# Sums and products of the Hyena spectra, the branch sums, the decay subtraction and the filter sums moved from GpSimd to VectorE

## The chip, the cores and the metric

The kernel runs on one core of one Trainium2 chip. A core has a TensorE (PE in the profile) for matmuls, a VectorE (DVE), a ScalarE (ACT), a GpSimd (POOL), and a SyncE (SP) that here issues most of the DMAs. Each engine works through its own queue in order, and semaphores hold an instruction back until what it reads is ready.

The metric is the device time of one launch in microseconds, the median of several runs. Lower is better.

## The reference

Two layers of an encoder trunk on 512 tokens of width 1024, in float32. Each layer does:

```
hn = RMSNorm(h);  u = hn @ w_in, cut into the parts of three branches and three gates
y_a = attention(q, k, v)          8 query heads, 2 key/value heads, rotary positions
y_b = hyena(v, x1, x2)            two long convolutions over 1024 points, by FFT
y_c = gated linear attention      4 heads, forward and backward, with decay gates
mixed = sum_i sigmoid(gate_i) * (y_i @ w_branch_i)
h = h + mixed @ w_out
h = h + cross_attention(RMSNorm(h), RMSNorm(mem))
h = h + relu(RMSNorm(h) @ w1)^2 @ w2
```

Four places of it matter here. The Hyena convolution multiplies spectra:

```
y = irfft(rfft(u, n=2L) * spec, n=2L)[:L] + u * skip
```

Its filter comes from a small sine network, is windowed, and is divided by the sum of its absolute values before its own rfft. The decay gates are `g = log_sigmoid(logit) / 16`, of which running sums are taken. And `mixed` is a sum over three branches.

## The kernel before

**Tiles.** Activations stand transposed, channels on the 128 partitions and the 512 tokens along the free axis, so most tiles are 128x512 float32. A matmul in float32 is made of three matmuls on rounded halves (`mm3`, L251 to L253): high by high, low by high, high by low. Every operand is split first: ScalarE rounds a copy (`split`, L235: wh, xh, pqh, mixh), and VectorE subtracts it from the source to get the low half (L236: wl, xl, pql, mixl). Weights arrive in chunks of 128x1024 (`wr`), two buffers of them, and are split the same way into `wh` and `wl`, three buffers each; so each weight chunk passes ScalarE and VectorE before TensorE can use it.

**Order.** A layer is written as generators (attention `at`, its projections and splits, `gp` and `gh` for gated linear attention, `hy0` and `hy1` for the two channel halves of Hyena, `ga` for gates, `me0`, `me1`, `me2` for merging a branch, `wo`, `kv`). A list of names (ORDER0, ORDER) says in which order their steps are traced. From the trace a planner with a model of costs makes each engine's queue; priorities shift it (weight splits are pulled 200 places ahead by SPLIT_AHEAD, some matmuls are pushed back by LATE). The queue of each engine is fixed before the launch. So an instruction that waits holds all that stand behind it on its engine.

**The lines that the change touches.**

- ENGS (L170) gives letters to a few groups of elementwise operations: V for VectorE, P for GpSimd. `engs(key)` turns them into engines. `fq` is used by `quarters` (L618 to L622) in the filters, `hq` by `quarters` in Hyena, `hp` in the spectral products (L823 to L826), `hi` in the inverse step (L830 to L838), `mx` in the norm ahead of the layer.
- `quarters` makes four tiles out of even and odd halves: one sum (L618), one difference (L619), and two tiles in two halves of 128x256 each (L622).
- `spectral` runs twice for each half of the channels, so eight times in all. In each of its four groups g it multiplies the tile by the filter's spectrum F, which comes from DRAM by a DMA, in four operations: two products of 128x512 (L823, L824) and a difference and a sum of 128x256 (L825, L826). Then sums and differences go back (L830 to L834) and four results (L838) are split for the matmuls of the inverse transform. With the letters of before, a call puts on GpSimd both halves of one tile of `quarters` (L622), the four operations of group 2, and two of the four L838.
- `filters` has four rounds a layer (two convolutions by two channel halves). A round adds and subtracts two halves of w3 (L673, L674, from `w3r`, one buffer, filled by a DMA), sums absolute values into `acc` (L711, three times a round), and ends in `quarters` (fq: L618 and L619 on GpSimd). In layer 0 the filters lie beside attention; those of layer 1 lie in the MLP of layer 0.
- `gla_proj` subtracts for each of four heads `g - c` (L965), and two scans on VectorE read the result (L966, L968). `c` comes from ScalarE in one piece for all four heads.
- `merge` multiplies the gate by the branch on VectorE (L1116), then adds it to `acc` (L1117), eight times for each of two branches a layer. After the last branch the sum is split (mixh, mixl) for w_out.

GpSimd does more than that: sums of squares for the norms (L352), the rotary sum (L452), part of the last MLP sums (L1376, L1377), small copies of the decay (L973 to L982), and the DMAs of the transform matrices.

Of the kernel before, what the change touches and what calls it, by code (L numbers as in the profile page):

```python
# [15 lines left out]
ALU = mybir.AluOpType  # L16
# [77 lines left out]
def laid_out(a):  # L94
# [43 lines left out]
    for s_ in range(2):  # L138
# [28 lines left out]
LATE = dict(ff=50, fn=100, fr=100, fs=50, gA=100, gm=35, go=150, gq=35, gs=150, gt=10, hc=100, ht=150,  # L167
            kt=300, pt=100, pv=150, qt=200, xs=200, xt=35, xv=10)

ENGS = dict(fq='PPVV', hq='VVPV', hp='VVPV', hi='VVVVPVPV', lx='VVVVVVVV', aw='V',  # L170
            mx='VPVPVPVP')
SMALL = 768

# [1 line left out]
class Trunk:  # L175
# [461 lines left out]
    def filters(self, l):  # L637

        nc, I = self.nc, self.I
# [24 lines left out]
        for o in range(2):  # L664
            rn = self.rnbuf[2 * (l % 2) + o]
            self.rn[l].append(rn)
            for c in range(2):


                raw = self.t("w3r", (P, 2, 256), F32, "w3r")  # L670
                self.load(raw, I["hy_w3"][l, o, c])
                wr = self.t("F", (P, 2, 256), F32, "w3s")
                nc.gpsimd.tensor_tensor(wr[:, 0], raw[:, 0], raw[:, 1], op=ALU.add)  # L673
                nc.gpsimd.tensor_tensor(wr[:, 1], raw[:, 0], raw[:, 1], op=ALU.subtract)  # L674
                wh = self.t("s12", (P, 2, 256), F32R, "w3h")
                for r in range(2):
                    nc.scalar.copy(wh[64 * r:64 * r + 64], wr[0:64])
# [6 lines left out]
                acc = self.t("s12", (P, 2, 256), F32, "acc")[:, 0]  # L684
                skip = self.skip
                self.load(skip, I["hy_skip"][l, o, c])
                for par in (1, 0):
                    win = self.t("win", (P, 2, 256), F32, "win")
                    self.load(win, I["c_win"][c, par])
                    T4 = []  # L690
                    for a in range(2):
                        tt = 2 * par + a
                        tk = slice(tt * P, (tt + 1) * P)
                        ps = self.ps("b", (P, 2, 256))
                        nc.tensor.matmul(ps, hs[:, tk], wh, start=True, stop=False)
                        nc.tensor.matmul(ps, hb[:, tk], wl, start=False, stop=True)
                        E = self.t("F", (P, 2, 256), F32, "eo")
                        nc.vector.tensor_tensor(E, ps, win[:, a].unsqueeze(1).to_broadcast([P, 2, 256]),
                                                op=ALU.mult)
                        if tt == 0:  # L700

                            nc.vector.tensor_tensor(tap0, E[0:1, 0], E[0:1, 1], op=ALU.add)
                            nc.vector.tensor_scalar(E[0:1], tap0.unsqueeze(1).to_broadcast([1, 2, 256]), 0.5,
                                                    None, op0=ALU.mult)

                        ab = self.t("F", (P, 2, 256), F32, "abs")
                        nc.scalar.activation(ab, E, AF.Abs)
                        top = acc if tt == 2 else ab[:, 0]
                        nc.vector.tensor_tensor(top, ab[:, 0], ab[:, 1], op=ALU.max)
                        if tt != 2:  # L710
                            nc.gpsimd.tensor_tensor(acc, acc, top, op=ALU.add)  # L711
                        eh, el = self.split_new(E, "f8", (P, 2, 256), "eo")
                        m = dft[par + 2 * a]


                        for x in range(1 + par):
                            bank = self.ps("a", (P, 2, 256))
                            for d in range(2):
                                with self.late("ff"):
                                    self.mm3(bank[:, d], m[:, d ^ x, 0], m[:, d ^ x, 1], eh[:, d], el[:, d],  # L720
                                             d == 0, d == 1 and tt > 0)
                            T4.append(bank)
                    if par == 1:
                        odd = [self.tile_sum("f8", T4[x], self.hold("f8", T4[2 + x]), (ALU.add, ALU.subtract)[x])
                               for x in range(2)]
                    else:
                        held = self.hold("f8", T4[1])
# [167 lines left out]
    def gla_proj(self, l):  # L895
# [66 lines left out]
        self.load(reset, I["c_reset"])  # L962
        for h in range(4):
            g, c = gs[h], xs[:, h]
            nc.gpsimd.tensor_tensor(g, g, c, op=ALU.subtract)  # L965
            nc.vector.tensor_tensor_scan(c[0:64], reset[0:64], g[0:64], 0.0,  # L966
                                         op0=ALU.mult, op1=ALU.add)
            nc.vector.tensor_tensor_scan(c[64:128, ::-1], reset[64:128, ::-1], g[64:128, ::-1],  # L968
# [132 lines left out]
    def merge(self, l, i, W, last):  # L1101
        nc = self.nc
        y = (self.ya, self.yb, self.yc)[i]
        for mc in range(4):
            w = self.wchunk(W[l], mc, ng=1)
            for j in range(2):
                m = 2 * mc + j
                py = self.ps("mm")
                self.proj_cm(py, w, slice(j * P, (j + 1) * P), y)
                t = self.gate[i][m]  # L1110
                if i == self.first:
                    a = self.t("h8", name="acc")
                    nc.vector.scalar_tensor_tensor(a, t, 1.0, py, op0=ALU.add, op1=ALU.mult)
                    self.acc.append(a)
                else:
                    nc.vector.scalar_tensor_tensor(t, t, 1.0, py, op0=ALU.add, op1=ALU.mult)  # L1116
                    nc.gpsimd.tensor_tensor(self.acc[m], self.acc[m], t, op=ALU.add)  # L1117
                if last:
                    self.mixed.append(self.split_new(self.acc[m], "g", name="mix", lo_tag="s12"))
            yield  # L1120
# [337 lines left out]
```

## Time and profile before

| | us |
|---|---|
| median of 3 runs | 2281.23 (2280.59 to 2283.82) |
| the profiled execution, whole | 2285.21 |
| its span in the trace | 2283.4 |
| GpSimd: L1117, 32 operations | 50.6 busy, 1.589 each |
| GpSimd: L838, 16 operations | 29.0 busy, 1.822 each |
| GpSimd: L823, 8 operations | 21.7 busy, 2.712 each |
| GpSimd: L711, 24 operations of 128x256 | 21.6 busy, 0.901 each |
| VectorE: weight splits L236, 324 of 128x1024 | 415.1 busy, 1.284 each |

How to read it: a profile is of one execution, and sums from its rows are held against that execution's time. Busy time is the time in which an engine had an instruction running. PE's is near the span, so what counts beside it is when PE has nothing to do. A row of the timeline has the start, the duration, the engine, the line, the operation, the tiles written and read, and their shapes; in brackets stands how long the engine had been idle before, and what ended that. On VectorE a duration includes a tail that overlaps the next instruction, so the distance between two starts is the price of one in a full queue.

### The profile page before, as it was taken

To read this page: it belongs to the slowest core of one execution; us is meant where nothing else is said; L and a number is where in the kernel's file an instruction comes from. 1 tells how busy PE (TensorE), PEld (TensorE's weight loads), DVE (VectorE), ACT (ScalarE), POOL (GpSimd) and SP (SyncE) were. 2 spreads that over 40 slices of the span, in tenths; PEclk is the share of its full clock that TensorE was granted. 3 is DMA by queue.
4 is the path that set the end of the run, shared out by engine and by line. 5 is a ranking of instruction groups with operands and counts; after the bars stand their busy time and mean duration, and the time that the engine had idled before them with its cause. 6 is when DMAs were issued, how large, how long until landed. Compare 5 with 4: busy or idle time off the path is not lost.

```text
span 2283.4 us, 28957 instructions
## 1 busy us (share of the span) xinstructions
PE 2197.6 (96%) x11032; PEld 1831.6 (80%) x11032; DVE 1533.5 (67%) x2455; ACT 1001.0 (44%) x1623; POOL 422.6 (19%) x353
## 2 busy tenths in 40 slices
PE   7989999998899999999999989999989999999999
PEld 5877888786678878888887878887867888888887
DVE  7798855979665765766485685667886566344445
ACT  6666844332344544443335576343323444433231
POOL 1142101224220101111060230102252101000004
PEclk9999999999999999999999999999989999999999
DMA  6442123223143243433344211332232322333332
GB/s 236 136 139 83 56 84 116 65 83 106 59 148 112 63 127 102 134 120 100 100 155 146 94 51 56 91 117 74 77 109 91 130 75 74 102 99 95 98 94 95
DMA packets 80098, 233.56 MB, mean 102 GB/s; under 512 B 9174, under 2 KB 11222, under 8 KB 79960
## 3 DMA queue, kind: packets, MB, share of 16 engines
q1 hardware_dynamic: 76792, 225.95, 31.2%
q0 software_dynamic: 3168, 5.77, 0.9%
q8 instruction: 86, 1.41, 0.3%
q14 instruction: 52, 0.43, 0.1%
HBM read 214.91 MB, written 16.78 MB: 101 GB/s over the span
## 4 chain that ended last, share of the span: by engine, by line
PE 78%; DVE 14%; issue 3%; ACT 2%; DMA 2%; POOL 1%; SPq 0%; DVEq 0%; POOLq 0%; ACTq 0%
PE ps L251 24%; PE ps L253 24%; PE ps L252 24%; DVE wl L236 3%; PE ps L557 1%; DVE ts L823 1%; ACT wh L235 1%; PE ps L566 1%; DMA F<-F 1%; PE ps L568 1%; DVE u L824 1%; PE ps L544 1%; DVE ts L611 1%; PE ps L545 0%; DMA wr<-in_w_in_dram 0%
## 5 line engine op out<-in xcount | busy, mean ns | idle before, releaser
L236 DVE TENSOR_TENSOR wl<-wr,wh 128x1024 fp32r<-128x1024 f32 x324 | 415.1, 1284 | 244.0 <-ACT wh L235 239.7
L235 ACT CAST wh<-wr 128x1024 fp32r<-128x1024 f32 (+1 forms) x328 | 341.0, 1042 | 507.1 <-PE ps L252 424.2
L253 PE MATMUL ps<-xh,wl 128*128 128x512 f32 x1344 | 530.6, 395 | 17.5 <-DVE wl L236 17.5
L251 PE MATMUL ps<-xh,wh 128*128 128x512 f32 x1344 | 532.9, 397 | 4.2 <-ACT wh L235 3.9
L252 PE MATMUL ps<-xl,wh 128*128 128x512 f32 x1344 | 531.1, 395 | 0.0
L253 PEld LDWEIGHTS ps<-xh,wl 128*128 128x128 f32 x1344 | 254.6, 189 | 73.8 <-DVE wl L236 22.5
L251 PEld LDWEIGHTS ps<-xh,wh 128*128 128x128 f32 x1344 | 254.8, 190 | 58.2 <-ACT wh L235 5.5
L252 PEld LDWEIGHTS ps<-xl,wh 128*128 128x128 f32 x1344 | 254.9, 190 | 50.0
L253 PE MATMUL ps<-hdh,wl 128*128 128x512 f32 x512 | 199.4, 390 | 0.0
L252 PE MATMUL ps<-hdl,wh 128*128 128x512 f32 x512 | 199.4, 390 | 0.0
L251 PE MATMUL ps<-hdh,wh 128*128 128x512 f32 x512 | 199.2, 389 | 0.0
L1374 DVE TENSOR_TENSOR macc<-ps,macc 128x512 f32<-128x512 f32 x96 | 65.9, 690 | 89.1 <-PE ps L253 88.9
L252 PEld LDWEIGHTS ps<-hdl,wh 128*128 128x128 f32 x512 | 96.1, 188 | 19.9
L253 PEld LDWEIGHTS ps<-hdh,wl 128*128 128x128 f32 x512 | 96.1, 188 | 19.8
L251 PEld LDWEIGHTS ps<-hdh,wh 128*128 128x128 f32 x512 | 96.1, 188 | 19.7
L1376 POOL TENSOR_TENSOR macc<-macc,rb 128x512 f32<-128x512 f32 x16 | 23.5, 1469 | 398.4 <-DVE macc L1374 398.4
L251 PE MATMUL ps<-wh,xh 128*128 128x256 f32 x320 | 91.7, 286 | 0.0
L252 PE MATMUL ps<-wl,xh 128*128 128x256 f32 x320 | 91.5, 286 | 0.0
L253 PE MATMUL ps<-wh,xl 128*128 128x256 f32 x320 | 91.1, 285 | 0.0
L1358 DVE TENSOR_TENSOR rl<-rl 128x512 f32<-128x512 f32 x64 | 44.6, 697 | 64.8 <-ACT rl L1357 64.8
L352 POOL TENSOR_TENSOR hsum<-hsum,hsq 128x512 f32<-128x512 f32 x30 | 43.6, 1454 | 168.3 <-ACT hsq L350 168.3
L1357 ACT ACTIVATE rl<-ps 128x512 f32<-128x512 f32 x64 | 37.9, 592 | 77.9 <-PE ps L253 77.9
(405 smaller groups left out, 4522.1 us busy)
## 6 DMA issues: line engine op xcount, KB each, us to landing
wr<-in_mlp_w_dram SPq DMA_DIRECT2D x128, 512.0 KB, 3.6
wr<-in_w_in_dram SPq DMA_DIRECT2D x108, 512.0 KB, 3.7
wraw<-in_x_wv_dram SPq DMA_DIRECT2D x16, 512.0 KB, 5.5
wr<-in_x_wk_dram SPq DMA_DIRECT2D x16, 512.0 KB, 3.7
F<-ff SPq DMA_DIRECT2D x32, 256.0 KB, 3.2
F<-F SPq DMA_DIRECT2D x32, 256.0 KB, 4.9
wr<-in_w_out_dram SPq DMA_DIRECT2D x16, 512.0 KB, 3.6
wr<-in_x_wq_dram SPq DMA_DIRECT2D x16, 512.0 KB, 3.7
```

The costliest lines, as they stand in the source:

```text
L235: r = self.nc.scalar.copy(hi, src)
L236: (lo_eng or self.nc.vector).tensor_tensor(lo, src, hi, op=ALU.subtract)
L251: mm(out, lh, rh, start=start, stop=False, skip_group_check=True)
L252: mm(out, lh, rl, start=False, stop=False, skip_group_check=True)
L253: mm(out, ll, rh, start=False, stop=stop, skip_group_check=True)
L352: eng.tensor_tensor(self.hsum, self.hsum, sq, op=ALU.add)
L544: nc.tensor.matmul(s, QH[:, tk], K2, start=True, stop=False)
L557: nc.tensor.transpose(pt[:, k, i * P:(i + 1) * P], Pn[i][:, (2 * kp + k) * P:(2 * kp + k + 1) * P], self.ident)
L1357: nc.scalar.activation(r, ps, AF.Relu)
L1358: nc.vector.tensor_tensor(r, r, r, op=ALU.mult)
L1374: nc.vector.tensor_tensor(acc[m], ps, acc[m], op=ALU.add)
L1376: nc.gpsimd.tensor_tensor(acc[m], acc[m], rb, op=ALU.mult)
```

## The change

All operations named above move from GpSimd to VectorE; nothing else is touched. The letters of `mx` stay as they are. Since the planner makes the queues from the whole program, the order on every engine may come out otherwise.

```diff
-ENGS = dict(fq='PPVV', hq='VVPV', hp='VVPV', hi='VVVVPVPV', lx='VVVVVVVV', aw='V',
+ENGS = dict(fq='VVVV', hq='VVVV', hp='VVVV', hi='VVVVVVVV', lx='VVVVVVVV', aw='V',
             mx='VPVPVPVP')
...
                 wr = self.t("F", (P, 2, 256), F32, "w3s")
-                nc.gpsimd.tensor_tensor(wr[:, 0], raw[:, 0], raw[:, 1], op=ALU.add)
-                nc.gpsimd.tensor_tensor(wr[:, 1], raw[:, 0], raw[:, 1], op=ALU.subtract)
+                nc.vector.tensor_tensor(wr[:, 0], raw[:, 0], raw[:, 1], op=ALU.add)
+                nc.vector.tensor_tensor(wr[:, 1], raw[:, 0], raw[:, 1], op=ALU.subtract)
...
                         if tt != 2:
-                            nc.gpsimd.tensor_tensor(acc, acc, top, op=ALU.add)
+                            nc.vector.tensor_tensor(acc, acc, top, op=ALU.add)
...
             g, c = gs[h], xs[:, h]
-            nc.gpsimd.tensor_tensor(g, g, c, op=ALU.subtract)
+            nc.vector.tensor_tensor(g, g, c, op=ALU.subtract)
...
                     nc.vector.scalar_tensor_tensor(t, t, 1.0, py, op0=ALU.add, op1=ALU.mult)
-                    nc.gpsimd.tensor_tensor(self.acc[m], self.acc[m], t, op=ALU.add)
+                    nc.vector.tensor_tensor(self.acc[m], self.acc[m], t, op=ALU.add)
```

## The prediction

> **What bounds the kernel now.** I read the page first: the busy shares and the chain that ended last.
>
> ```profile
> span 2283.4 us, 28957 instructions
> PE 2197.6 (96%) x11032; PEld 1831.6 (80%) x11032; DVE 1533.5 (67%) x2455; ACT 1001.0 (44%) x1623; POOL 422.6 (19%) x353
> PE 78%; DVE 14%; issue 3%; ACT 2%; DMA 2%; POOL 1%; SPq 0%; DVEq 0%; POOLq 0%; ACTq 0%
> ```
>
> TensorE (PE) works 2197.6 of 2283.4 us. No matmul is added or removed, so almost all that an edit elsewhere can gain lies in the 85.8 us in which PE idles and in what those pauses do to its clock. VectorE (DVE) is busy only 67% on average, which says little; hence the stages next. The view of windows gives, per stretch, its length and then the busy time of PE, PEld, DVE, ACT and POOL, the granted clock and the DMAs. The four stretches are attention with the filters of layer 0, Hyena of layer 0, Hyena of layer 1, and the last merge of layer 1.
>
> ```profile
> 60.00:300.00 240.00, 223.60 (x1363) 193.14 (x1362) 207.60 (x394) 163.48 (x314) 60.96 (x69) 0.98 0.32 103
> 410.00:600.00 190.00, 173.91 (x857) 144.66 (x855) 158.50 (x228) 58.20 (x86) 57.45 (x38) 0.96 0.25 78
> 1535.00:1725.00 190.00, 175.94 (x867) 146.61 (x866) 155.64 (x226) 57.50 (x83) 59.78 (x38) 0.96 0.26 81
> 1725.00:1780.00 55.00, 51.17 (x219) 39.36 (x218) 34.95 (x40) 20.39 (x28) 17.91 (x11) 0.97 0.34 111
> ```
>
> PE idles 16.1 us in the first Hyena stretch and 14.1 us in the second (length less PE), more than a third of all its idleness, and there DVE is busy 83%. What PE waits for stands in the timeline of PE, in brackets behind the matmul that was late:
>
> ```profile
> 433.68 0.50 PE L253 MATMUL ps<-xh,wl 128*128 128x512 f32 x1 [2.71 <-DVE wl L236]
> 539.82 0.80 PE L251 MATMUL ps<-zh,dft 128*128 128x256 f32 x2 [4.43 <-ACT zh L235]
> 580.40 0.80 PE L253 MATMUL ps<-yah,wl 128*128 128x512 f32 x1 [3.94 <-DVE wl L236]
> 1310.57 0.50 PE L253 MATMUL ps<-xh,wl 128*128 128x512 f32 x1 [1.39 <-DVE wl L236]
> 1560.98 0.50 PE L253 MATMUL ps<-xh,wl 128*128 128x512 f32 x1 [2.66 <-DVE wl L236]
> 1673.30 0.79 PE L253 MATMUL ps<-ych,wl 128*128 128x512 f32 x1 [4.57 <-DVE wl L236]
> 1706.77 0.80 PE L253 MATMUL ps<-yah,wl 128*128 128x512 f32 x1 [3.88 <-DVE wl L236]
> 1768.29 0.50 PE L251 MATMUL ps<-mixh,wh 128*128 128x512 f32 x1 [2.20 <-ACT mixh L235]
> ```
>
> Six of these pauses lie in Hyena, 22.2 us together; five wait for the low half of a weight split (wl, L236) that stands on DVE behind the spectral arithmetic. So the question is what the change does to DVE's queue ahead of those splits. The timelines of DVE and of POOL ahead of the 4.57 us pause:
>
> ```profile
> 1660.49 1.78 DVE L823 TENSOR_TENSOR ts<-u,F 128x512 f32<-128x512 f32 x1
> 1662.19 1.51 DVE L826 TENSOR_TENSOR held<-ts 128x256 f32<-128x256 f32 x1
> 1663.62 1.77 DVE L824 TENSOR_TENSOR u<-u,F 128x512 f32<-128x512 f32 x1
> 1665.32 1.22 DVE L823 TENSOR_TENSOR ts<-u,F 128x512 f32<-128x512 f32 x1
> 1666.46 0.96 DVE L825 TENSOR_TENSOR u<-u 128x256 f32<-128x256 f32 x1
> 1669.55 0.68 DVE L831 TENSOR_TENSOR ts<-held,u 128x512 f32<-128x512 f32 x1
> 1670.15 0.68 DVE L832 TENSOR_TENSOR ts<-held,u 128x512 f32<-128x512 f32 x1
> 1670.76 0.41 DVE L833 TENSOR_TENSOR ts<-held,u 128x256 f32<-128x256 f32 x1
> 1671.09 0.41 DVE L834 TENSOR_TENSOR ts<-u,held 128x256 f32<-128x256 f32 x1
> ```
>
> ```profile
> 1660.22 1.50 POOL L823 TENSOR_TENSOR ts<-held,F 128x512 f32<-128x512 f32 x1 [1.85 <-DMA F<-F]
> 1661.68 1.74 POOL L1117 TENSOR_TENSOR acc<-acc,gt 128x512 f32<-128x512 f32 x1
> 1663.38 1.47 POOL L824 TENSOR_TENSOR held<-held,F 128x512 f32<-128x512 f32 x1
> 1664.93 1.06 POOL L825 TENSOR_TENSOR held<-held 128x256 f32<-128x256 f32 x1
> 1666.06 1.07 POOL L826 TENSOR_TENSOR held<-ts 128x256 f32<-128x256 f32 x1
> ```
>
> The reader is to see two things. With POOL silent (from 1669.55) a 128x512 sum of two SBUF tiles takes DVE 0.68 us and the next one starts 0.60 us later; a 128x256 one takes 0.41 and 0.33. With POOL at work (1660 to 1667) the same operations take 1.78, 1.51, 1.77, 1.22 and 0.96: 1.10 + 1.10 + 1.09 + 0.54 + 0.55 = 4.4 us more, for five POOL operations. The two engines get in each other's way; an operation on POOL costs DVE more than if DVE did it.
>
> **The change part by part.** From the letters and loops, 160 operations move: 88 of 128x512 (32 of L1117, 16 of L838, 8 each of L618, L619, L823, L824, L965) and 72 of 128x256 (24 of L711, 16 of L622, 8 each of L825, L826, L673, L674). At 0.60 and 0.33 us that is 88 x 0.60 + 72 x 0.33 = 77 us more in DVE's queue. No DMA moves and no operation disappears.
>
> *Spectral arithmetic and the sums of branches inside Hyena.* In the chain above the five operations take DVE 3 x 0.60 + 2 x 0.33 = 2.5 us, and the 4.4 us go: the split behind them comes 1.9 us sooner. I take 1.9 us for each of the six pauses, all at least 2.6 us long: -11.4 us. For a whole stretch: its 38 POOL operations (22 wide, 16 narrow) cost DVE 22 x 0.60 + 16 x 0.33 = 18.5 us, and free 22 x 1.1 + 16 x 0.54 = 32.8 us if every one collides. That bounds the two stretches together between -28.6 us (but not beyond the pauses' 22.2) and, if nothing collided, +37. Break-even is at 18.5/32.8 = 56% colliding; in the chain shown all five do, so I stay with that row.
>
> [...]
>
> *The clock.* After a long pause PE restarts slowly: of two equal matmuls in the timeline of PE behind the 4.57 us pause, the first comes soon after it and the second 4.7 us later.
>
> ```profile
> 1674.32 0.63 PE L252 MATMUL ps<-ycl,wh 128*128 128x512 f32 x1
> 1679.04 0.39 PE L252 MATMUL ps<-ycl,wh 128*128 128x512 f32 x1
> 1673.00:1675.00 2.00, 1.70 (x4) 1.41 (x5) 0.24 (x1) 0.60 (x2) 2.00 (x2) 0.50 0.38 70
> ```
>
> The third row is the window of the first: the granted clock was 0.50 there, and the second matmul is back at its usual length. Some 4 us at half clock lose about 2 us. The pauses of 4.43, 3.94, 4.57 and 3.88 us can each bring this; cut by 1.9 they are near the 2.66 and 2.71 us ones, whose first matmuls above take 0.50, not 0.80. At most 8 us; I take half, -4, as the length from which the clock falls is not known from these rows.
>
> *Decay gates (L965).* Three subtractions on POOL, the DVE operations beside them, and a scan without them:
>
> ```profile
> 1304.66 4.77 POOL L965 TENSOR_TENSOR mn<-mn,ab 128x512 f32<-128x512 f32 x3 [16.30 <-ACT ab L958]
> 1305.99 2.30 DVE L966 TENSOR_TENSOR_SCAN ab<-reset,mn 64x512 f32<-64x512 f32 x1 [7.07 <-POOL mn L965]
> 1308.21 4.67 DVE L236 TENSOR_TENSOR wl<-wr,wh 128x1024 fp32r<-128x1024 f32 x2
> 1312.92 1.22 DVE L968 TENSOR_TENSOR_SCAN ab<-reset,mn 64x512 f32<-64x512 f32 x1
> 1672.03 1.21 DVE L236 TENSOR_TENSOR wl<-wr,wh 128x1024 fp32r<-128x1024 f32 x1
> ```
>
> The scan loses 1.08 us and the two splits 4.67 - 2 x 1.21 = 2.2 us; four subtractions on DVE add 2.4. With the first scan starting some 0.6 us sooner (1.33 us after the subtraction's start now, 0.68 then) a layer gains about 1.5 us, no more than the 1.39 us pause nearby: -1.3 us a layer, -2.5 in all, bounds 0 and -5.
>
> *Last merge (L1117 ahead of the w_out operands).* The 2.20 us pause waits for mixh, a cast of the sum that POOL makes:
>
> ```profile
> 1765.47 2.11 POOL L1117 TENSOR_TENSOR acc<-acc,gt 128x512 f32<-128x512 f32 x1 [2.43 <-DVE gt L1116]
> ```
>
> 2.11 becomes 0.68: -1.4 us there. DVE has room in that stretch (34.95 of 55), which hides the other sums. Bounds -3 and +2; I take -1.5 for both layers.
>
> *Filters (L618, L619, L673, L674, L711).* In layer 1 they lie in the MLP, where PE does not wait. In layer 0 they fall in the first stretch, 207.6 of 240 us of DVE. Four rounds of two wide and five narrow operations add 4 x (1.20 + 1.65) = 11.4 us.
>
> ```profile
> 118.56 3.60 DVE L622 TENSOR_TENSOR ff<-ts,ts 128x256 f32<-128x256 f32 x4
> POOL w3s L673 <- DMA w3r<-in_hy_w_dram: 56.7, 2, 29.3
> ```
>
> The first row, beside L618 and L619 on POOL, would take 4 x 0.33 alone, so a round frees 2.2 us, 8.8 in all. Net +2.6 us in DVE's queue; I take +2, bounds 0 and +6. The second row (from the view of waits: engine and line, what it waited for, us in total, times, longest) is a new wait: POOL could sit idle for w3r, DVE cannot, as splits and the sine's operations queue behind L673. The order is laid out by a planner that knows of the load, and two loads only were waited for; within the +6.
>
> *Order.* The planner lays out all queues anew. No row prices that; I bound it by one long pause with its clock loss, 4.57 + 2, either way, and take 0.
>
> Sum: -11.4 - 4 - 2.5 - 1.5 + 2 = -17.4 us, against the profiled execution's 2285.2 us (its span of 2283.4 and 1.8 around it). That execution lies 4.0 above the median of 2281.2, so 2281.2 - 17.4 = **2264 us**.
>
> **The rivals.**
> 1. *Clean sweep:* the pauses in Hyena vanish, with their clock loss: -22.2 - 8, with decay and merge -2.5 - 1.5, and filters +2: 2249 us. [...] Against it: five of the six pauses end with a split that still has a whole round of spectral operations ahead of it.
> 2. *Even:* the collisions free what the moved work adds, or the pauses pass to the next wait, such as the loads of F or the casts on ACT. Against it: the queue shown is DVE's own for 14 us without a break. Only decay and merge remain, eaten by the filters: 2280 us.
> 3. *Slower, by a full VectorE:* fewer than 56% of the moved operations in Hyena collide, since much of the POOL work falls beside VectorE operations on PSUM. At 35% a stretch frees 11.5 us and adds 18.5, and its splits come 7 us later. Two stretches give +14, and with the other terms, -2.5 - 1.5 + 2, 2293 us. For it: DVE is the late engine and gets 77 us more. Against it: the five of five in the chain. [...]
>
> **How the numbers follow.** Forecast 0.57, clean sweep 0.13, even 0.14, slower 0.16. A measurement of this kernel tells about 0.2%, 4.6 us, from no change. Faster is forecast and sweep, 0.70; within it 0.14; slower 0.16. The range leaves out about a tenth at each end: below, the better half of the sweep's case (2245); above, most of the slower one (2286), so that it takes in the even case and the unknown order.
>
> **What would show it.** In the profile after, POOL's busy time falls from 422.6 to about 180 us (160 operations at 1.54 us, the mean of the 76 in the Hyena stretches), and the spectral operations on DVE read 0.68 and 0.41 us throughout. DVE's busy time stays near 1533 us, within 30. PE's pauses in Hyena fall from 30 us to under 20, none over 3.5 us, and the clock there rises above 0.96. It is wrong if those pauses stay while DVE's operations are short (the next wait took over), if DVE's busy time rises by 50 us (few collided), or if pauses appear in the first stretch.

## The result, and the profile after

The changed kernel takes **2229.41 us** (median of 4 runs, 2224.12 to 2232.6); the kernel before, run beside it, 2282.53 (median of 4 runs, 2280.59 to 2284.9). The ratio is **0.9765**, with a 95% interval of 0.9743 to 0.9786: 53 us less, where 17 were forecast. The time lies below the forecast's range (2245 to 2286). The profiled execution took 2230.03 us.

The page of the kernel after: span, busy times, the shares of the chain that ended last, and two groups (busy us, mean ns of one, idle time of the engine just before, and what ended it).

```profile
span 2228.3 us, 28873 instructions
PE 2181.0 (98%) x11032; PEld 1824.3 (82%) x11032; DVE 1532.3 (69%) x2615; ACT 1003.8 (45%) x1623; POOL 197.1 (9%) x193
PE 83%; DVE 6%; ACT 3%; DMA 2%; issue 1%; ACTq 0%; DVEq 0%; SPq 0%
L236 DVE TENSOR_TENSOR wl<-wr,wh 128x1024 fp32r<-128x1024 f32 x324 | 402.2, 1242 | 250.9 <-ACT wh L235 245.5
L253 PE MATMUL ps<-xh,wl 128*128 128x512 f32 x1344 | 527.5, 393 | 3.3 <-DVE wl L236 3.1
```

The last group in the kernel before, from its view of lines:

```profile
L253 PE MATMUL ps<-xh,wl 128*128 128x512 f32 x1344 | 530.6, 395 | 17.5 <-DVE wl L236 17.5
```

VectorE got 160 operations more and is as busy as before (1532.3 against 1533.5 us). PE's wait for late weight splits in the largest group of matmuls fell from 17.5 to 3.1 us.

The span is 55.1 us shorter. Two parts make that up, by the two pages: PE idles 2228.3 - 2181.0 = 47.3 us instead of 85.8, which is 38.5 less, and the same 11032 matmuls keep it busy 16.6 us less. The windows of the kernel after (columns as in the prediction) show where the idle time went. Hyena of layer 1 comes earlier now, so its window starts at 1500.

```profile
60.00:300.00 240.00, 229.44 (x1396) 199.12 (x1395) 211.97 (x428) 166.68 (x319) 24.04 (x34) 0.99 0.33 105
410.00:600.00 190.00, 184.61 (x921) 153.79 (x920) 159.96 (x273) 64.35 (x91) 0.00 (x0) 1.00 0.29 89
1500.00:1690.00 190.00, 187.51 (x965) 156.60 (x964) 165.66 (x285) 67.45 (x98) 0.00 (x0) 1.00 0.29 89
```

Length less PE busy gives 5.4 and 2.5 us of idle time in the two Hyena windows, where it was 16.1 and 14.1, and 10.6 in attention with the filters, where it was 16.4. The granted clock in Hyena is 1.00 instead of 0.96. The longest pauses that are left in Hyena of layer 0 (first two rows) and elsewhere, from the timeline of PE after:

```profile
523.89 0.51 PE L251 MATMUL ps<-zh,dft 128*128 128x256 f32 x2 [1.99 <-ACT zh L235]
...
588.61 0.73 PE L251 MATMUL ps<-ybh,wh 128*128 128x512 f32 x2 [1.54 <-ACT ybh L235]
...
1172.36 0.80 PE L252 MATMUL ps<-wl,mnh 128*128 128x512 f32 x1 [3.02 <-DVE wl L236]
...
1298.58 1.22 PE L544 MATMUL ps<-k,qh 128*128 128x512 f32 x2 [2.40 <-ACT qh L532]
```

Neither of Hyena's two waits for a weight split any more. What changed ahead of the splits is to be seen in the timeline of VectorE after:

```profile
1624.74 0.42 DVE L826 TENSOR_TENSOR held<-ts 128x256 f32<-128x256 f32 x1
1625.08 0.69 DVE L824 TENSOR_TENSOR u<-u,F 128x512 f32<-128x512 f32 x1
1625.68 0.69 DVE L830 TENSOR_TENSOR ts<-held,u 128x512 f32<-128x512 f32 x1
1626.28 0.42 DVE L825 TENSOR_TENSOR u<-u 128x256 f32<-128x256 f32 x1
1626.61 0.69 DVE L831 TENSOR_TENSOR ts<-held,u 128x512 f32<-128x512 f32 x1
1627.32 1.23 DVE L236 TENSOR_TENSOR wl<-wr,wh 128x1024 fp32r<-128x1024 f32 x1
1628.46 0.42 DVE L826 TENSOR_TENSOR u<-ts 128x256 f32<-128x256 f32 x1
```

Every spectral operation takes its undisturbed 0.69 or 0.42 us, and the planner has put a weight split between two operations of one call.

**The clock.** The matmuls are the same, and in the prediction's rows one of two equal ones took 0.63 us at a granted clock of 0.50 and 0.39 later. So the 16.6 us of busy time are held against the clock. The mean granted clocks, from the view of cores, before and after:

```profile
core 0: 2283.4 us, clock 0.985
```

```profile
core 0: 2228.3 us, clock 0.993
```

By these, (1 - 0.985) x 2283.4 = 34.3 us were lost before and (1 - 0.993) x 2228.3 = 15.6 after: 18.7 less, near the 16.6 of PE's busy time. It need not be the same, for the mean counts a low clock in PE's pauses too. Where it was lost before is seen in windows of 10 us, one at each of the six long pauses in Hyena:

```profile
430.00:440.00 10.00, 7.29 (x32) 5.51 (x31) 8.18 (x13) 4.24 (x6) 4.11 (x2) 0.83 0.19 56
540.00:550.00 10.00, 9.95 (x39) 8.01 (x40) 8.87 (x15) 1.68 (x2) 2.88 (x2) 0.76 0.13 32
580.00:590.00 10.00, 9.60 (x38) 7.80 (x39) 7.02 (x12) 3.46 (x6) 3.52 (x2) 0.71 0.25 80
1560.00:1570.00 10.00, 9.02 (x35) 7.27 (x36) 7.99 (x14) 4.24 (x6) 3.30 (x2) 0.83 0.34 107
1670.00:1680.00 10.00, 6.70 (x20) 5.35 (x21) 8.19 (x14) 3.43 (x5) 5.45 (x3) 0.66 0.18 54
1700.00:1710.00 10.00, 6.12 (x21) 4.47 (x20) 8.59 (x16) 1.78 (x3) 2.61 (x2) 0.77 0.36 102
```

These six windows lose 1.7 + 2.4 + 2.9 + 1.7 + 3.4 + 2.3 = 14.4 us. That is an estimate of what PE lost: some of it lies in the pauses themselves, and the last window ends before the clock is back. The first and the fourth belong to the shorter pauses (2.71 and 2.66 us). Windows of 1 us show when the clock fell: behind the first pause, which ended at 433.68, behind the fourth, which ended at 1560.98, and inside the second (4.43 us long, ended at 539.82).

```profile
434.00:435.00 1.00, 1.00 (x9) 0.97 (x8) 0.00 (x0) 0.21 (x1) 1.00 (x2) 1.00 0.39 49
435.00:436.00 1.00, 1.00 (x5) 0.78 (x4) 0.56 (x1) 1.00 (x2) 1.00 (x1) 0.79 0.74 283
...
1561.00:1562.00 1.00, 1.00 (x8) 0.96 (x9) 0.00 (x0) 0.00 (x0) 1.00 (x1) 0.99 0.09 33
1562.00:1563.00 1.00, 1.00 (x4) 0.85 (x4) 0.25 (x1) 0.90 (x2) 1.00 (x2) 0.50 0.75 217
...
538.00:539.00 1.00, 0.00 (x0) 0.00 (x0) 1.00 (x3) 0.00 (x0) 1.00 (x1) 0.50 0.00 0
```

Behind the two shorter pauses the clock falls 1.9 and 1.0 us after PE has started again, so the first matmul does not show it. In the longer one it fell while PE still paused.

### The profile page after: what moved, and what is told of

Read it like the earlier page. It is cut to its first block, busy times and chain, and to the rows that moved or that the text cites. A ratio compares the mean times of both kernels' runs of the same rounds, so it can differ in the third digit from the quotient of the medians.

```text
span 2228.3 us, 28873 instructions
## 1 busy us (share of the span) xinstructions
PE 2181.0 (98%) x11032; PEld 1824.3 (82%) x11032; DVE 1532.3 (69%) x2615; ACT 1003.8 (45%) x1623; POOL 197.1 (9%) x193
## 4 chain that ended last, share of the span: by engine, by line
PE 83%; DVE 6%; ACT 3%; DMA 2%; issue 1%; ACTq 0%; DVEq 0%; SPq 0%
PE ps L251 26%; PE ps L253 25%; PE ps L252 25%; DVE wl L236 2%; PE ps L557 1%; ACT wh L235 1%; PE ps L566 1%; PE ps L568 1%; DMA wr<-in_w_in_dram 1%; PE ps L544 1%; ACT p L549 1%; DMA wr<-in_w_br_gla_dram 1%; PE ps L545 1%; PE ps L1312 0%; DVE ab L968 0%
## 5 line engine op out<-in xcount | busy, mean ns | idle before, releaser
L236 DVE TENSOR_TENSOR wl<-wr,wh 128x1024 fp32r<-128x1024 f32 x324 | 402.2, 1242 | 250.9 <-ACT wh L235 245.5
L352 POOL TENSOR_TENSOR hsum<-hsum,hsq 128x512 f32<-128x512 f32 x30 | 43.3, 1445 | 602.4 <-ACT hsq L350 602.4
L1376 POOL TENSOR_TENSOR macc<-macc,rb 128x512 f32<-128x512 f32 x16 | 23.5, 1467 | 651.1 <-DVE macc L1374 651.1
```

The source lines that it names most:

```text
L236: (lo_eng or self.nc.vector).tensor_tensor(lo, src, hi, op=ALU.subtract)
L352: eng.tensor_tensor(self.hsum, self.hsum, sq, op=ALU.add)
L1376: nc.gpsimd.tensor_tensor(acc[m], acc[m], rb, op=ALU.mult)
```

## The experiments

All eighteen, with the median of the kernel before that ran beside each. Busy times are from the pages. The changed kernel itself is the row "after".

| label | us | before | ratio (95%) | DVE busy | PE busy |
|---|---|---|---|---|---|
| after | 2229.41 | 2282.53 | 0.9765 (0.9743 to 0.9786) | 1532.3 | 2181.0 |
| e1_only_spectral | 2253.43 | 2283.82 | 0.9867 (0.9851 to 0.9884) | 1520.6 | 2187.8 |
| e5_late_fill | 2246.95 | 2284.04 | 0.9837 (0.982 to 0.9854) | 1491.8 | 2180.7 |
| e13_spec_left_out | 2248.97 | 2282.19 | 0.9858 (0.9841 to 0.9874) | 1494.7 | 2181.3 |
| e2_port_read | 2253.2 | 2283.82 | 0.9866 (0.9851 to 0.9882) | 1562.6 | 2186.5 |
| e3_port_write | 2231.16 | 2283.82 | 0.9766 (0.9749 to 0.9783) | 1533.4 | 2180.8 |
| e6_dve_extra | 2246.07 | 2284.04 | 0.9828 (0.9805 to 0.985) | 1563.5 | 2187.1 |
| e7_only_filters | 2277.93 | 2284.04 | 0.9971 (0.9961 to 0.998) | 1538.2 | 2197.2 |
| e8_only_decay | 2271.53 | 2284.04 | 0.9949 (0.9932 to 0.9966) | 1526.0 | 2200.2 |
| e10_decay_fill | 2278.99 | 2282.51 | 0.9988 (0.9978 to 0.9998) | 1526.1 | 2192.8 |
| e14_decay_left_out | 2274.79 | 2282.19 | 0.9972 (0.9961 to 0.9983) | 1525.8 | 2194.8 |
| e9_only_merge | 2270.19 | 2282.51 | 0.9947 (0.9932 to 0.9962) | 1540.5 | 2190.2 |
| e15_merge_left_out | 2294.6 | 2282.19 | 1.0054 (1.0039 to 1.0069) | 1516.5 | 2197.7 |
| e16_before_ahead210 | 2284.05 | 2284.04 | 1.0002 (0.9993 to 1.0011) | 1531.1 | 2200.4 |
| e17_before_ahead204 | 2288.16 | 2284.04 | 1.0019 (1.001 to 1.0028) | 1532.9 | 2197.5 |
| e18_after_ahead204 | 2232.16 | 2284.04 | 0.9774 (0.9761 to 0.9788) | 1532.3 | 2178.9 |
| e4_all_vector | 2241.97 | 2283.82 | 0.9819 (0.98 to 0.9838) | 1547.5 | 2183.4 |
| e11_decay_small | 2229.36 | 2282.51 | 0.9765 (0.9751 to 0.978) | 1537.0 | 2177.9 |
| e12_mlp_tail | 2230.04 | 2282.51 | 0.9766 (0.9752 to 0.9781) | 1539.6 | 2181.1 |

Gains below are ratios times the time of before, so that the medians of different chips do not mix.

### The spectral arithmetic: moved, made harmless, left out

```diff
-ENGS = dict(fq='PPVV', hq='VVPV', hp='VVPV', hi='VVVVPVPV', ...
+ENGS = dict(fq='PPVV', hq='VVVV', hp='VVVV', hi='VVVVVVVV', ...
```

> Only the letters of hq, hp and hi become V; filters, decay subtraction and branch sums stay on GpSimd. Theory 1 (collisions: an operation on GpSimd takes more of VectorE's time than it saves, and the weight splits stand behind it): the spectral part is most of the gain, 25 to 40 us of the 53, so 2242 to 2257 us. Theory 2 (GpSimd's results came late and the order of VectorE's queue, laid out anew over all five parts, brings the weight splits forward): the spectral letters alone give under half, 2260 to 2275 us.

It gains 30 us by itself.

In the next kernel the same eight operations of a call stay on GpSimd, but each becomes three fills, which read nothing; and in the third they are gone, so nothing waits for them either.

```diff
-                eng.tensor_tensor(m2, x, f[g][:, ::-1], op=ALU.mult)
+                self.fill(eng, m2, x, f[g][:, ::-1], ALU.mult)
...
+    def fill(self, eng, out, x, y, op):
+        if eng is not self.nc.gpsimd:
+            eng.tensor_tensor(out, x, y, op=op)
+        else:
+            for _ in range(3):
+                eng.memset(out, 0.0)
```

> The kernel before, but in the spectral calls the eight operations that GpSimd has are replaced by fills with zeros of the same tiles (three fills each, 1.6 us for a wide one and 0.9 for a narrow one by the run with fills), so part of the convolution is left out. GpSimd's results come about as late as before, the chain of waits stays, VectorE gets no new work, but GpSimd no longer reads beside it. Theory 1 (collisions): some 24 us, what the sums of a constant tile gave back, are gained: 2255 to 2263 us. Theory 2 (GpSimd's late results hold the chain): it stays within 10 us of the kernel before, 2274 to 2284.

```diff
-                eng.tensor_tensor(m2, x, f[g][:, ::-1], op=ALU.mult)
+                self.skip_pool(eng, m2, x, f[g][:, ::-1], ALU.mult)
...
+    def skip_pool(self, eng, out, x, y, op):
+        if eng is not self.nc.gpsimd:
+            eng.tensor_tensor(out, x, y, op=op)
```

> The kernel before without the eight operations that GpSimd has in each spectral call, so part of the convolution is left out; no collision, no late result and no new work on VectorE. If lateness counts beside collisions (37 us without them), it is 8 to 14 us faster than the run with fills, 2233 to 2239 us, and the 30 us of work then cost 14 to 20 us in the run that moved the spectral letters. If fills had already freed all, it is within 4 us of them, 2243 to 2251, and the work cost only some 6 us.

Fills gain 37 us, leaving out 32. Their intervals overlap, so these two runs show no price for VectorE's waits for GpSimd's results. (The fills wait for less than the operations did, not for F for one, so they do not come as late as was expected of them.) The page of e5_late_fill gives the price of the collisions:

```profile
PE 2180.7 (97%) x11032; PEld 1821.8 (81%) x11032; DVE 1491.8 (66%) x2455; ACT 1002.6 (45%) x1623; POOL 398.9 (18%) x481
```

With as many operations on VectorE as before (x2455) it is busy 1533.5 - 1491.8 = 41.7 us less: that is what these 64 operations cost it. If each collided, by the prediction's 1.1 and 0.54 us it would be 32 x 1.1 + 32 x 0.54 = 52.5, so 79% did. And the 41.7 us were worth 37 of time, 0.9 each. The moved work, 32 x 0.60 + 32 x 0.33 = 29.8 us by the prediction's prices, shows in e1_only_spectral as 1520.6 - 1491.8 = 28.8. It gave back only 37 - 30 = 7 us, 0.2 each. Against e13_spec_left_out it makes VectorE 25.9 us busier and costs 2 us, 0.1 each.

### The collision put back, and the same work on VectorE

To the changed kernel each spectral call adds eight sums of a constant tile on GpSimd. Nobody reads the result. A copy of four columns starts them where the old operations stood.

```diff
+            ...; self.busy(u[2][:, 0, 0:4], (256, 256, 512, 512, 256, 256))
...
+            ...; self.busy(a[:, 0, 0:4], (512, 512))
...
+    def busy(self, ready, cols):
+        self.nc.gpsimd.tensor_copy(self.junk[:, 0:4], ready)
+        for c in cols:
+            j, s = self.junk[:, 0:c], self.idle[:, 0:c]
+            self.nc.gpsimd.tensor_tensor(j, s, s, op=ALU.add)
```

> The changed kernel, and beside each of the eight spectral calls GpSimd makes eight sums (four of 128x512, four of 128x256, as many as were moved away) of a constant tile into a scratch tile that nobody reads; a copy of four columns starts them as the spectra come. VectorE's work and nearly all of its order stay. Theory 1 (collisions): VectorE loses up to 64 operations at 1.1 and 0.54 us, 52 us, and half or more of what the change gained comes back as pauses of TensorE: 2250 us or more. Theory 2 (lateness and order): nothing waits for these sums, so under 10 us come back, 2229 to 2239 us, although the operations beside them read 1.2 to 1.8 us.

The second does the same with fills of about the same time; only the operation is another.

```diff
-            self.nc.gpsimd.tensor_tensor(j, s, s, op=ALU.add)
+            for _ in range(3 if c == 512 else 2):
+                self.nc.gpsimd.memset(j, 0.0)
```

> As the kernel before this one, but GpSimd fills the scratch tile with zeros (three fills for a wide sum, two for a narrow one) in place of the sums, so that it is busy and writes, but reads nothing. If the collision is over reading two tiles, VectorE's operations stay at 0.68 and 0.41 us and the time at that of the changed kernel, 2225 to 2234 us. If any work of GpSimd slows VectorE, it comes out as the kernel with sums.

Groups of e2_port_read: the wide sums on GpSimd, then VectorE operations in the window from 410 to 600 us, which take 0.685 us undisturbed.

```profile
L1436 POOL TENSOR_TENSOR consts<-consts 128x512 f32<-128x512 f32 x32 | 41.3, 1292 | 2.5
```

```profile
L823 DVE TENSOR_TENSOR ts<-u,F 128x512 f32<-128x512 f32 x8 | 8.0, 999 | 0.8 <-DMA F<-F 0.8
L824 DVE TENSOR_TENSOR held<-held,F 128x512 f32<-128x512 f32 x8 | 8.0, 998 | 0.0
```

A group of e3_port_write, the fills:

```profile
L1437 POOL MEMSET consts<- 128x512 f32 x96 | 50.6, 528 | 5.5
```

Sums that read make VectorE busy 30.3 us longer and give back (0.9866 - 0.9765) x 2283.8 = 23 us of the gain, 0.8 for each; fills give back nothing and leave VectorE at 1533.4. No result depends on either, so this is the collision. (The order is not quite the same: 287 of PE's 11032 matmuls stand elsewhere in the one than in the other. Nudges of that size, below, moved the time by at most 4 us.) So in these two runs it was GpSimd operations that read that collided: the fills, which only write, cost VectorE 1533.4 - 1532.3 = 1.1 us.

What GpSimd takes by itself is to be seen where VectorE is idle beside it, in the kernel before:

```profile
166.97 0.72 POOL L711 TENSOR_TENSOR acc<-acc,abs 128x256 f32<-128x256 f32 x1
622.46 1.30 POOL L1117 TENSOR_TENSOR acc<-acc,gt 128x512 f32<-128x512 f32 x1 [4.54 <-DVE gt L1116]
```

So 256 elements more take it 0.58 us. In the prediction's rows VectorE lost 0.54 or 0.55 us beside a narrow operation and 1.10 beside a wide one. The five GpSimd operations in those rows took 1.50 + 1.74 + 1.47 + 1.06 + 1.07 = 6.8 us; undisturbed they would take 3 x 1.30 + 2 x 0.72 = 5.3, an estimate from the two rows above.

The third puts the constant sums on VectorE.

```diff
-        self.nc.gpsimd.tensor_copy(self.junk[:, 0:4], ready)
+        self.nc.vector.tensor_copy(self.junk[:, 0:4], ready)
...
-            self.nc.gpsimd.tensor_tensor(j, s, s, op=ALU.add)
+            self.nc.vector.tensor_tensor(j, s, s, op=ALU.add)
```

> The changed kernel, with the sums of a constant tile of the run with sums made by VectorE instead: 64 operations at 0.60 and 0.33 us and sixteen copies of four columns, about 31 us more in VectorE's queue, and no collision. If every microsecond in VectorE's queue in Hyena costs the same, whatever it is made of, this comes back like the 30 us of collisions did, +18 to +28: 2247 to 2257 us. If such work mostly falls into VectorE's idle time and only stretched operations hurt, under +12: below 2241.

VectorE is busy 31.2 us longer, and (0.9828 - 0.9765) x 2284 = 14 us are lost, 0.5 for each. So extra work is not free, but costs less than as much time in collisions. Neither figure is sharp: by the ends of the intervals this one lies between 0.1 and 0.8, and that of e1 against e5 between 0 and 0.5.

### Filters alone

The filter letters (fq), L673, L674 and L711 on VectorE, everything else as before.

```diff
-ENGS = dict(fq='PPVV', ...
+ENGS = dict(fq='VVVV', ...
...
-                            nc.gpsimd.tensor_tensor(acc, acc, top, op=ALU.add)
+                            nc.vector.tensor_tensor(acc, acc, top, op=ALU.add)
```

> Only the filters move (fq, w3's sum and difference, the sums of absolute values). By the prediction's step +2 us, 2279 to 2287. If the filters carry a part of what the spectral letters did not give (23 us), it is 5 us or more faster than before, under 2278, and the place to look is TensorE's pauses between 120 and 240 us.

It gains 6.6 us, though VectorE is busy 4.7 us longer. A loss was forecast. By its page PE idles 2278.8 - 2197.2 = 81.6 us instead of 85.8; which of the moved operations shortened which pause was not traced, so the cause stays open.

### Decay alone: moved, filled, left out

```diff
-            nc.gpsimd.tensor_tensor(g, g, c, op=ALU.subtract)
+            nc.vector.tensor_tensor(g, g, c, op=ALU.subtract)
```

> Only the subtraction of the decay gates moves. By the prediction's step -2.5 us, 2277 to 2283. If the decay stage carries a large part of the rest, TensorE's pauses of 1.39, 0.96, 1.82 and 3.82 us between 1310 and 1334 go and it is 6 to 12 us faster, 2271 to 2277.

```diff
-            nc.gpsimd.tensor_tensor(g, g, c, op=ALU.subtract)
+            for _ in range(3): nc.gpsimd.memset(g, 0.0)
```

> The kernel before, with the subtraction of the decay gates on GpSimd replaced by three fills of the same tile, so the decay's minimum is left out of the sums. GpSimd's queue stays as long (about 1.6 us a head ahead of the small copies), but it does not read beside VectorE's scans and splits. If collisions make the 12 us of the run that moved the subtraction, most of them come here too: 2270 to 2276 us. If the queue of GpSimd, in which the small copies stand behind the subtractions of later heads, makes them, it stays within 4 us of before: 2279 to 2285.

```diff
-            nc.gpsimd.tensor_tensor(g, g, c, op=ALU.subtract)
+            pass
```

> The kernel before without the subtraction of the decay gates. With the fills 3 us were gained, with the move 12. If the subtractions hold up the small copies behind them in GpSimd's queue, leaving them out gives what the move gave or more, 12 to 16 us: 2266 to 2270. If it was the new order that came with the move, leaving them out gives little more than the fills: 2275 to 2281.

Moved 11.6 us, filled 2.7, left out 6.4; the intervals of the last two overlap. The windows where the decay lies (attention of layer 0, then layer 1), in the kernel before:

```profile
100.00:300.00 200.00, 183.60 (x1132) 158.42 (x1131) 178.63 (x331) 137.17 (x266) 55.61 (x61) 0.97 0.30 95
1280.00:1400.00 120.00, 111.09 (x677) 95.66 (x676) 93.26 (x139) 85.70 (x167) 29.42 (x29) 0.97 0.18 56
```

and in e8_only_decay:

```profile
100.00:300.00 200.00, 191.41 (x1188) 165.46 (x1186) 177.81 (x343) 140.45 (x271) 48.50 (x57) 0.99 0.31 100
1280.00:1400.00 120.00, 115.99 (x693) 99.61 (x693) 95.86 (x145) 90.12 (x177) 16.59 (x23) 0.97 0.20 60
```

PE idles 7.8 and 4.9 us less there, 12.7 together. Over the whole span PE's busy time is 2.6 us longer, and the execution profiled is 9.9 us shorter in its span. Of what came sooner, the part on GpSimd is this. Before:

```profile
1304.66 4.77 POOL L965 TENSOR_TENSOR mn<-mn,ab 128x512 f32<-128x512 f32 x3 [16.30 <-ACT ab L958]
1309.38 1.18 POOL L973 COPY small<-ab 64x4 f32<-64x4 f32 x1
1310.53 1.28 POOL L965 TENSOR_TENSOR mn<-mn,ab 128x512 f32<-128x512 f32 x1
1314.27 1.10 POOL L974 COPY small<-ab 64x4 f32<-64x4 f32 x1 [2.47 <-DVE ab L968]
...
1321.70 3.57 POOL L982 TENSOR_TENSOR small<-small 128x4 f32<-128x4 f32 x1
```

In e8_only_decay:

```profile
1305.42 1.10 POOL L973 COPY small<-ab 64x4 f32<-64x4 f32 x1 [21.10 <-DVE ab L966]
1306.67 1.10 POOL L974 COPY small<-ab 64x4 f32<-64x4 f32 x1
...
1311.81 0.54 POOL L982 TENSOR_TENSOR small<-small 128x4 f32<-128x4 f32 x1
```

The subtractions stood in GpSimd's queue ahead of the small copies (L973, L974), of which the second came 9.6 us after the first subtraction's start (1304.66 to 1314.27); in e8_only_decay it comes 6.1 us after the first subtraction on VectorE, whose row is this:

```profile
1300.60 1.29 DVE L965 TENSOR_TENSOR mn<-mn,ab 128x512 f32<-128x512 f32 x2 [5.70 <-ACT ab L958]
```

The fills do not settle whether that delay or the collision counts, as was expected of them. They do not read ScalarE's result (`ab`, L958), so they run long before it is there, and the small copies come sooner too. In e10_decay_fill:

```profile
1296.20 3.10 POOL L965 MEMSET mn<- 128x512 f32 x6 [10.04 <-DVE mn L954]
...
1305.04 1.17 POOL L974 COPY small<-ab 64x4 f32<-64x4 f32 x1
```

The second small copy starts there 9.2 us sooner than in the kernel before. So the kernel with fills and the one without the subtraction are both rid of the collision, and no subtraction stands ahead of the copies; yet they gain only 2.7 and 6.4 us. What gives the other 5 to 9 us of the move, these runs do not tell, and the intervals of moving and leaving out still overlap a little. The new order around it is one candidate.

### The branch sums alone: moved, left out

```diff
-                    nc.gpsimd.tensor_tensor(self.acc[m], self.acc[m], t, op=ALU.add)
+                    nc.vector.tensor_tensor(self.acc[m], self.acc[m], t, op=ALU.add)
```

> Only the sums of branches (L1117) move. The other four parts gave 30, 6 and 12 us one by one, of 53; if the parts add up, this one gives about 5 us: 2275 to 2281. By the prediction's step (1.5 us at the last merge, the ones inside Hyena counted with the spectra) 2 to 4 us. If it is 0 or slower, the parts help one another instead.

```diff
-                    nc.gpsimd.tensor_tensor(self.acc[m], self.acc[m], t, op=ALU.add)
+                    pass
```

> The kernel before without the sums of branches (L1117), so only the first branch reaches the output. If their collisions and lateness on GpSimd cost what the spectral ones do (0.58 us each by the fills), 32 of them cost some 19 us, of which the move to VectorE gives some 8 back: 2260 to 2267 us. If the move's 12 us came from pauses that fell below the length from which the clock drops, and not from the operations themselves, it gains no more than the move: 2268 to 2274.

Moved, they gain 12 us, although VectorE is busy 7 us longer (1540.5). The 32 sums add 32 x 0.60 = 19.2, so they freed about 12 of the 32 x 1.1 = 35 us that full collision would free, 35%. PE's busy time falls by 7.4 us, and the granted clock of the profiled execution is 0.989 instead of 0.985, so a good part of the gain is clock. In its timeline the four long pauses of Hyena are 3.95, 2.75, 3.01 and 3.22 us, 12.9 together, where they were 16.8. Left out, the kernel is 12 us slower, with 32 operations fewer and none more. No theory had that. The timeline of PE of e15_merge_left_out shows two pauses that the kernel before does not have:

```profile
599.72 0.58 PE L251 MATMUL ps<-pqh,dft 128*128 128x256 f32 x1 [9.11 <-ACT pqh L235]
...
620.94 1.22 PE L251 MATMUL ps<-ybh,wh 128*128 128x512 f32 x2 [8.18 <-ACT ybh L235]
```

Its GpSimd ahead of the first one:

```profile
596.18 4.07 POOL L838 TENSOR_TENSOR held<-ts,ts 128x512 f32<-128x512 f32 x2 [7.39 <-DVE ts L832]
```

In this order the next matmul in PE's queue is one of the inverse transform, and its operand comes from the first of two spectral operations on GpSimd, which had waited for L832 on VectorE. These two pauses, 17.3 us, are more than the whole loss. So this kernel does not price the sums. That an unlucky order made the pauses is argued from these rows, and no other run tests it.

### The order alone

One number of the planner, in the kernel before twice and in the changed one; by the traces, 278, 107 and 298 of PE's 11032 matmuls (compared by line and tiles, in the order of their starts) then stand elsewhere than in their own kernel.

```diff
-SPLIT_AHEAD = 200
+SPLIT_AHEAD = 210
```

> The kernel before with its weight splits pulled 210 places ahead in the planner instead of 200; every operation stays on its engine, only the queues come out in another order. Theory A (a new order alone moves the time by 5 to 12 us, so single-part gains of 6 to 12 us cannot be split between engine and order): it differs from before by 5 us or more, either way. Theory B (order alone is worth little, the single parts' gains are the moves' own): within 3 us of before, 0.9987 to 1.0013.

> The kernel before with its weight splits pulled 204 places ahead instead of 200, a smaller change of the order. Theory A: one of the two nudged kernels of before differs from it by 5 us or more. Theory B: both within 3 us.

> The changed kernel with its weight splits pulled 204 places ahead instead of 200. Theory A: 5 us or more from the changed kernel's ratio of 0.9765, either way. Theory B: within 3 us of it. A third reading: the changed kernel has little idle time left and so depends less on the order than the kernel before, and it stays within 3 us though before does not.

0, +4 and +2 us. Neither theory is clean, but no nudge makes 12 us. By the same count e9_only_merge and e1_only_spectral move 77 and 147 matmuls of the kernel before, no more than the nudges do, and gain 12 and 30 us. e7_only_filters and e8_only_decay move 414 and 412, more than any nudge, so their 6.6 and 11.6 us are less safely the moves' own. e15_merge_left_out, with 276, loses 12 us without any added work, so an order may be worth more than these nudges were.

### Further on the same way

Most of the elementwise work that is left on GpSimd moves to VectorE too (L352, L408, L452, a low half in L1008, L1010, L1266, L1376, L1377):

```diff
-            nc.gpsimd.tensor_tensor(dst, u, v, op=ALU.add)
+            nc.vector.tensor_tensor(dst, u, v, op=ALU.add)
...
-                    nc.gpsimd.tensor_tensor(sqs, sqs, sq, op=ALU.add)
+                    nc.vector.tensor_tensor(sqs, sqs, sq, op=ALU.add)
```

> The changed kernel with the rest of GpSimd's sums and products on VectorE too (sums of squares, rotary sum, norm products, the low half of v, k by the decay, the last MLP products); only copies of four columns, fills and DMAs stay. Theory 1: the remaining collisions outside Hyena, some 50 us of VectorE's time, go, but TensorE pauses little there, so 0 to 8 us faster, 2221 to 2230. Rival: VectorE, now with 70 us more of its own work around attention, is late there and the time is 5 to 15 us above that of the changed kernel.

It loses (0.9819 - 0.9765) x 2283.8 = 12 us against the changed kernel. By the pages PE idles 57.1 us instead of 47.3. Among the new pauses are two in cross attention, one a layer:

```profile
739.57 1.69 PE L1312 MATMUL ps<-consts,xp 128*128 128x128 f32 x6 [3.71 <-DVE xp L1308]
...
1843.42 0.77 PE L1312 MATMUL ps<-consts,xp 128*128 128x128 f32 x4 [3.71 <-DVE xp L1308]
```

Only the small copies of the decay (L973 to L982), and only the last MLP sums (L1376, L1377):

```diff
-            nc.gpsimd.tensor_copy(mid[0:64], c[0:64, 63::P])
+            nc.vector.tensor_copy(mid[0:64], c[0:64, 63::P])
```

> The changed kernel, with the five small operations of each head (copies of four columns and their product) on VectorE as well. They take 0.5 to 1.2 us on GpSimd beside a busy VectorE, in a chain that TensorE waits for (2.40 us at 1298). If it is their lateness, 2 to 6 us faster than the changed kernel, 2223 to 2228; if VectorE's queue is what counts there, no change within 2 us.

```diff
-                        nc.gpsimd.tensor_tensor(acc[m], acc[m], rb, op=ALU.mult)
+                        nc.vector.tensor_tensor(acc[m], acc[m], rb, op=ALU.mult)
```

> The changed kernel, with the two operations of GpSimd on the last MLP sums (L1376, L1377) on VectorE; the order of TensorE and ScalarE stays. They stretch VectorE's operations by some 30 us in two places where TensorE does not wait, so if only stretched operations behind which TensorE waits count, no change: 2226 to 2233. If every collision costs, 5 to 15 us faster.

Neither differs from the changed kernel, and no version here beats it. The second moves 32 operations of 128x512, 32 x 0.60 = 19.2 us, and VectorE is busy only 7.3 us longer, so some 12 us of collisions went, and no time was gained. In these two places, where TensorE does not wait, collisions had no price.

## Why the prediction was off

The mechanism was the one forecast, and the direction; nearly every term was too small. Of the 55.1 us by which the span fell, 22.3 are idle time of PE in the two Hyena windows (11.4 forecast), 16.2 are idle time elsewhere (2.5 + 1.5 - 2 = 2 forecast), and 16.6 are shorter busy time of PE, the clock (4 forecast).

- **What bounds the kernel, and the collision:** as forecast. e2_port_read against e3_port_write shows the collision. The five GpSimd operations of the prediction's chain took 6.8 us while VectorE lost 4.4; undisturbed they would take about 5.3, much nearer to the 4.4. Of the signs named, all came: GpSimd's busy time fell to 197.1 us (about 180 forecast), the spectral operations read 0.69 and 0.42, VectorE's busy time moved by 1.2 us, idle time in Hyena fell from 30.2 to 7.9 (under 20 forecast), the clock there rose to 1.00.
- **Hyena, "I take 1.9 us for each of the six pauses": the step that failed first.** Idle time fell by 22.3 us instead of 11.4; the clean sweep's figure of 22.2 was right. For GpSimd's late results the runs show no price (e5 gained 37 us, e13 32). The step charged each added microsecond on VectorE like one freed. Measured in Hyena, a microsecond of collision cost 0.8 to 0.9 us of time (e2, e5), one of added work 0.1 to 0.2 (e1 against e13 and e5) or 0.5 (e6). A reading that would explain it, argued and not shown: the planner's costs hold the added work, so it sets the splits ahead of it, as in the timeline after; it places nothing with regard to collisions.
- **The clock, "at most 8 us; I take half": the second step that failed.** The loss fell by some 17 us. The prediction knew a slow clock by a slow first matmul behind the pause and so counted four of six pauses. All six paid, 14.4 us together by the windows. Behind the two shorter ones the clock fell 1.9 and 1.0 us after PE had restarted; the four longer ones lost more than the 8 us it took as the most (2.4 + 2.9 + 3.4 + 2.3 = 11, part of it in the pauses), and half of that was left out. The prediction reasoned with a length of pause from which the clock falls; no run shows one (rows in the last section), nor what sets the delay.
- **Decay, -2.5:** 11.6 alone. The sum had the collisions and the start of one scan. It left out that the subtractions stood ahead of GpSimd's small copies. But a kernel rid of the subtraction altogether gains 6.4, so by the medians collision and delay together do not explain the 11.6, and what does stays open. Of PE's idle time in the first window, 7.8 us of 16.4 went with this move.
- **Branch sums, -1.5 (with those inside Hyena counted there):** 12 alone, with PE's busy time 7.4 us shorter, so here too the clock was missed. Some 3.9 us of the 12 are shorter pauses in Hyena, which the prediction counted under Hyena. Only 35% of the possible collisions were there, below the 56% at which the prediction set break-even, and it still gained. So that threshold was no threshold of the time.
- **Filters, +2:** 6.6 gained alone. VectorE's 4.7 us more were forecast about right (2.6 a layer in its queue); that this delays PE was wrong. Why it gained instead was not traced.
- **Order, 0 with 6.6 either way:** three nudges moved the time by 0 to 4 us, within the bound. e15_merge_left_out lies beyond it.
- **Slower by a full VectorE:** that VectorE operations on PSUM do not collide, as it assumed, the traces show: L611 (ts<-ps,held) took 0.683 us on average before and 0.684 after, while L823 on SBUF tiles (ts<-u,F) took 1.158 before and 0.685 after. The loss it forecast was wrong here, but not far off on the same way: e4_all_vector loses 12 us with VectorE only 15 us busier, by waits in other stages.

The four parts alone add up to 30.4 + 11.6 + 12.1 + 6.6 = 60.7 us, and together give 53. The parts share pauses, and the difference was not traced further.

## What to carry to other kernels

Where sums and products on GpSimd stand beside VectorE operations on SBUF tiles, as here, price an operation on GpSimd by what it takes from VectorE (64 of them took 41.7 us in the spectral calls), and find the price with one kernel in which fills stand in GpSimd's place: if VectorE's busy time falls, the collision is there. Price a pause of TensorE with the clock behind it, read over the next 10 us and not from the next matmul. Added work on VectorE cost less than its length here (0.1 to 0.5 us of time for each), and collisions ahead of splits that TensorE waited for cost nearly all of theirs (0.8 to 0.9). When an operation is replaced to find its price, look in the trace whether the replacement still waits for the same results. Stop moving when the waits come from other stages, as they did in the last step here.

## What the hardware showed that was not expected

- Fills on GpSimd of 50.6 us (96 of 128x512) beside VectorE's two-input operations cost it nothing: 1533.4 us busy with them, 1532.3 without.
- An operation of 128x4 took 3.57 us on GpSimd (L982 at 1321.70, shown above). VectorE ran four operations without a break meanwhile, the last of which ended at 1325.20, and the small one ended 0.07 us later. The other seven of L982 in that trace took 0.20 to 0.72 us, so a small operation can be delayed far beyond its size.
- Pauses of 2.66 and 2.71 us were each followed by half clock (granted 0.50), 1.0 and 1.9 us after PE had restarted, at a cost of 1.7 us each. The length of the pause alone does not decide: one of 2.40 us, ending at 133.22, brought no half clock, and the half clock from 1452.8 to 1459.6 follows no pause of 0.9 us or more in the 10 us before it. In the kernel before, each of the 13 stretches of half clock that ended within the span lasted 3.41 or 6.83 us.
- A kernel with 32 sums fewer was 12 us slower (ratio 1.0054, 1.0039 to 1.0069).
